# Storing two rows of the last tile in groups of partitions, so that one DMA engine takes half as many of them

## The chip, the cores and the metric

One core of a Trainium2 chip runs the whole kernel. The metric is the device time of one execution in microseconds (us); smaller is better. The kernel before took 3724.84 us (median of the fast runs). The profile counts 16 DMA engines for the core, whose packets move all the data between the chip's memory (HBM) and the core's own memory (SBUF): 1610.68 MB on the page of the kernel before.

## The reference

```python
# x, residual: (32, 2048, 2048) float32; gamma: (2048,), eps: a number
def reference(x, residual, gamma, eps):
    z = x + residual
    rms = np.sqrt(np.mean(z ** 2, axis=-1, keepdims=True) + eps)
    return (z / rms * gamma).astype(np.float32)
```

There are 65,536 rows of 8192 bytes. x and residual are read once and the result is written once: 1.61 GB.

## The kernel before

The rows are cut into tiles of 128 partitions times R = 7 rows (the first two tiles hold 3 and 5). SyncE's queue loads x and stores the results, ScalarE's queue loads the residual, VectorE adds and scales, ScalarE squares and sums. The last tile is done in four pieces of 2, 2, 2 and 1 rows, so that its stores can start early:

```python
    z = [sb(f"z{p}", [P, R, D]) for p in range(2)]
    tail = [(0, 2), (2, 4), (4, 6), (6, 7)]
    # ... (tiles, adds, squares, scaling)
    def sync_program(sp):
        # ... (loads and stores of all tiles but the stores of the last)
        for k, (a, b) in enumerate(tail):
            sp.wait_ge(tail_ev["done"], k + 1)
            sp.dma_start(
                out=rows(o_f, last)[:, a:b, :], in_=z[last % 2][:, a:b, :]
            ).then_inc(s_tail, U)
    # ...
    nc.gpsimd.wait_ge(ev["s_out"][(last - 1) % 2], ((last - 1) // 2 + 1) * U)
    nc.gpsimd.wait_ge(s_tail, U * len(tail))
    # ... (GpSimd clears the semaphores, and the program ends)
```

## Time and profile before

| | before |
|---|---|
| time, median | 3724.84 us |
| span of the profiled execution (which took 3725.53 us) | 3723.7 us |
| share of time in which the 16 DMA engines are busy | 100% |
| last 57344-byte packet of the second-last tile ends | 3705.04 us |
| last completion write of any engine | 3722.13 us |
| last of the 64 landings of the tail's stores | 3722.59 us |

The kernel is limited by the DMA engines from its first microseconds to about 3716 us. What can be gained at the end is the stretch in which engines fall idle one after another. The prediction below shows these lines of the profile and reads them. This is the view of all instructions that write the result tensor, from 3690 us on. After the name stand the count, the shortest, median and longest duration in ns, and the first and last start:

```profile
L269 SPq DMA_DIRECT2D out_dram<-z x4: 332/332/344, 3690.4 to 3708.8; - x4
```

### The profile page before, as it was taken

Reading aid. Unit: us, or ns where it says so; the run is one execution under the profiler, and the core shown is the slowest. Engines: PE = TensorE matmul, PEld = TensorE weight load, DVE = VectorE, ACT = ScalarE, POOL = GpSimd, SP = SyncE. Lnnn points to the kernel's source line nnn. Section 1 sums busy time; section 2 is a strip of 40 time slices with the busy share of each in tenths; the row PEclk is TensorE's granted clock in tenths of the full one; section 3 lists DMA queues with packets and bytes.
Section 4 is the critical chain, followed back from the end, with each engine's and each line's share of the span. In section 5 each row is a group of like instructions: output and inputs, shape, how many; then the busy total and the mean of one; then the engine's idle time right before and its main releaser. Section 6 shows DMA issues by size and latency. Waiting matters only on the chain.

```text
span 3723.7 us, 3798 instructions
## 1 busy us (share of the span) xinstructions
DVE 2302.6 (62%) x816; ACT 1072.4 (29%) x1176; POOL 0.2 (0%) x4
## 2 busy tenths in 40 slices
DVE  5666665566665566665566665566665566665566
ACT  2233322233322233322233322233322233322233
POOL 0000000000000000000000000000000000000000
DMA  9999999999999999999999999999999999999999
GB/s 421 431 434 435 434 434 435 434 435 435 434 434 434 434 434 434 434 434 433 434 434 434 434 434 434 434 434 434 434 434 434 434 434 434 434 434 434 434 432 398
DMA packets 32963, 1610.68 MB, mean 433 GB/s; under 512 B 3712, under 2 KB 3776, under 8 KB 3776
## 3 DMA queue, kind: packets, MB, share of 16 engines
q1 hardware_dynamic: 22592, 1082.17, 67.2%
q10 hardware_dynamic: 10368, 528.49, 32.8%
q14 instruction: 3, 0.02, 0.0%
HBM read 1073.77 MB, written 536.87 MB: 433 GB/s over the span
## 4 chain that ended last, share of the span: by engine, by line
DMA 67%; DVE 22%; issue 9%; ACT 2%; SPq 0%; DVEq 0%; ACTq 0%
DMA out_dram<-z 39%; DMA z<-in_x_dram 27%; DVE z L172 15%; DVE z L177 7%; ACT sq_junk L223 1%; ACT rms L231 0%; DVE rstd L197 0%; SPq L259 0%; DVEq L127 0%; DVE r_area L275 0%; ACTq L211 0%; ACTq L127 0%; SPq L141 0%; DVE tail_rstd L292 0%; SPq L162 0%
## 5 line engine op out<-in xcount | busy, mean ns | idle before, releaser
L172 DVE TENSOR_TENSOR z<-z,r_area 128x8192 f32<-128x8192 f32 (+2 forms) x150 | 1109.5, 7437 | 1252.5 <-DMA z<-in_x_dram 1252.5
L223 ACT ACTIVATE sq_junk<-z 128x2048 f32<-128x2048 f32 x512 | 963.4, 1882 | 2617.1 <-DVE z L172 2605.7
L177 DVE SCALAR_TENSOR_TENSOR z<-z,rstd,gamma_tile 128x2048 f32<-128x2048 f32 x505 | 1153.6, 2344 | 5.2
L197 DVE RECIPROCAL rstd<-rms 128x4 f32<-128x4 f32 (+2 forms) x146 | 25.3, 173 | 130.8 <-ACT rms L231 130.8
L223 ACT ACTIVATION_READ_ACCUMULATOR sq_junk<-z 128x1 f32 x512 | 95.5, 186 | 0.0
L231 ACT ACTIVATE rms<-ssq,eps_tile 128x4 f32<-128x4 f32 (+2 forms) x146 | 43.3, 297 | 13.4
L177 DVE SCALAR_TENSOR_TENSOR z<-z,tail_rstd,gamma_tile 128x2048 f32<-128x2048 f32 x7 | 16.2, 2345 | 0.1
L277 DVE LOAD_MASK_SELECT gamma_tile<-r_area x1 | 0.0, 14 | 16.1 <-DMA r_area<-in_gamma_dram 16.1
L277 DVE STREAM_SHUFFLE gamma_tile<-r_area 128x2048 f32<-128x2048 f32 x1 | 2.3, 2290 | 0.0
L275 DVE MEMSET r_area<- 128x2048 f32 x1 | 1.8, 1765 | 0.4 <-issue 0.4
L223 ACT ACT_TABLE_LOAD x1 | 1.3, 1283 | 0.9 <-SPq L77 0.9
L231 ACT ACT_TABLE_LOAD x1 | 1.3, 1283 | 0.1
L231 ACT ACTIVATE tail_rms<-tail_ssq,eps_tile 128x2 f32<-128x2 f32 (+1 forms) x4 | 1.2, 295 | 0.1
L274 DVE MEMSET eps_tile<- 128x1 f32 x1 | 0.1, 59 | 1.0 <-SPq L77 1.0
L292 DVE RECIPROCAL tail_rstd<-tail_rms 128x2 f32<-128x2 f32 (+1 forms) x4 | 0.6, 158 | 0.0
L349 POOL MEMSET const-bfloat16-1.0<- 128x1 bf16 x1 | 0.1, 101 | 0.0
L349 POOL MEMSET const-uint8-127<- 128x1 uint8 x1 | 0.1, 101 | 0.0
L349 POOL MEMSET const-float32-0.0<- 128x1 f32 x1 | 0.1, 98 | 0.2 <-issue 0.2
L349 POOL MEMSET const-float32-1.0<- 128x1 f32 x1 | 0.1, 98 | 0.0
## 6 DMA issues: line engine op xcount, KB each, us to landing
r_area<-in_residual_dram ACTq DMA_DIRECT2D x72, 7168.0 KB, 35.5
z<-in_x_dram SPq DMA_DIRECT2D x71, 7168.0 KB, 27.5
out_dram<-z SPq DMA_DIRECT2D x71, 7168.0 KB, 40.8
z<-in_x_dram SPq DMA_DIRECT2D x3, 2048.0 KB, 17.9
out_dram<-z SPq DMA_DIRECT2D x3, 2048.0 KB, 15.0
r_area<-in_residual_dram SPq DMA_DIRECT2D x1, 5120.0 KB, 25.0
z<-in_x_dram SPq DMA_DIRECT2D x1, 5120.0 KB, 36.7
out_dram<-z SPq DMA_DIRECT2D x1, 5120.0 KB, 26.5
```

The source lines that it names most:

```text
L172: return v.tensor_add(out=s, in0=s, in1=r_area[:, e + a : e + b, :])
L177: ins = v.scalar_tensor_tensor(out=s, in0=s, scalar=rs[:, c + g - a : c + g - a + 1], in1=gamma_tile[:, :], op0=mult, op1=mult,)
L197: v.reciprocal(out=rstd[p][h][:, :n], in_=rms[p][h][:, :n]).then_inc(dve, U)
L223: s.activation(out=sq_junk[:, :], in_=src[:, g, :], func=Act.Square, accum_out=sq[:, g - a : g - a + 1],)
L231: return s.activation(out=rm, in_=sq[:, : b - a], func=Act.Sqrt, bias=eps_tile[:, :], scale=inv_d)
L274: v.memset(eps_tile[:, :], float(eps))
L275: v.memset(stage, 0.0).then_inc(tail_ev["add"], 1)
L277: v.stream_shuffle(gamma_tile[:, :].rearrange("p (a b) -> p a b", a=16), stage, [0] * 32)
L292: v.reciprocal(out=tail_rstd[:, a:b], in_=tail_rms[:, a:b]).then_inc(dve, U)
L349: nc = _bacc.Bacc("TRN2", target_bir_lowering=False, num_devices=1)
```

## The change

One DMA engine ends some 3 us after all others (its last completion write is at 3722.13 us, that of any other at 3718.97 or before). The change takes work off it: rows 1 and 3 of the last tile are no longer stored over all 128 partitions. SyncE stores them for partitions 0 to 39 in ten small groups of 5, 4, 3 or 1 partitions, and GpSimd for 40 to 127 in two groups of 44. A small group runs on few engines: SyncE's load of k partitions has k landings, for k = 1 to 8. The trace doesn't number engines; number k - 1 in this document is the one that the load of k partitions adds. The sum is meant to give engine 4 eight rows less than it had. Two tiny loads on GpSimd's queue go ahead of its two stores.

```diff
+    tiny = sb("tiny", [8, 32])
+    soft = [sem(f"soft{k}") for k in range(4)]
 ...
-        for k, (a, b) in enumerate(tail):
+        for k, (a, b) in enumerate([(0, 1), (2, 3), (4, 6), (6, 7)]):
             sp.wait_ge(tail_ev["done"], k + 1)
-            sp.dma_start(
-                out=rows(o_f, last)[:, a:b, :], in_=z[last % 2][:, a:b, :]
-            ).then_inc(s_tail, U)
+            store_last(sp, slice(0, P), slice(a, b)).then_inc(s_tail, U)
+            if k == 1:
+                for q in low:
+                    store_last(sp, q, slice(1, 4, 2)).then_inc(s_tail, U)
+
+    low = [slice(k, k + 33, 8) for k in range(4)] + [slice(k, k + 25, 8) for k in range(4, 8)]
+    low += [slice(36, 39), slice(39, 40)]
+    high = [slice(k, P, 2) for k in (40, 41)]
+    n_tail = 4 + len(low)
+
+    def store_last(eng, q, r):
+        return eng.dma_start(out=rows(o_f, last)[q, r, :], in_=z[last % 2][q, r, :])
+
+    def pool_program(g):
+        def two_pairs(t, k):
+            return t[:5, 16 * k : 16 * k + 16].rearrange("p (a b) -> p a b", a=2)[:, :, :2]
+        for k in range(2):
+            g.dma_start(out=two_pairs(tiny, k), in_=two_pairs(x_f, k)).then_inc(soft[2 * k], U)
+            if k == 0:
+                g.wait_ge(tail_ev["done"], 2)
+            store_last(g, high[k], slice(1, 4, 2)).then_inc(soft[2 * k + 1], U)
+        for k in soft:
+            g.wait_ge(k, U)
+        g.dma_reset(range(soft[0].num, soft[-1].num + 1))
 ...
-    nc.gpsimd.wait_ge(s_tail, U * len(tail))
+    nc.gpsimd.wait_ge(s_tail, U * n_tail)
```

More of the change, by code (lines that the diff above doesn't have):

```diff
@@ L54 @@
     HI = LO + 2 * n_iter
-    assert n_iter >= 1
+    assert n_iter >= 1 and P == 128
     def rows(t, i):
@@ L326 @@
     scalar_program(nc.scalar)
+    pool_program(nc.gpsimd)
     nc.gpsimd.wait_ge(ev["s_out"][(last - 1) % 2], ((last - 1) // 2 + 1) * U)
-    nc.gpsimd.wait_ge(s_tail, U * len(tail))
+    nc.gpsimd.wait_ge(s_tail, U * n_tail)
     ids = [a.num for a in sems]
```

## The prediction

> **What bounds the kernel now.** I read the page first, then the busy time by stretches around the end, then the waits of SyncE's queue, then the single DMA packets and semaphore updates that the trace holds. The page's head, its DMA rows and its queues:
>
> ```profile
> span 3723.7 us, 3798 instructions
> DVE 2302.6 (62%) x816; ACT 1072.4 (29%) x1176; POOL 0.2 (0%) x4
> DMA  9999999999999999999999999999999999999999
> GB/s 421 431 434 435 434 434 435 434 435 435 434 434 434 434 434 434 434 434 433 434 434 434 434 434 434 434 434 434 434 434 434 434 434 434 434 434 434 434 432 398
> q1 hardware_dynamic: 22592, 1082.17, 67.2%
> q10 hardware_dynamic: 10368, 528.49, 32.8%
> ```
>
> No compute engine is near its limit, and the two queues together keep the 16 DMA engines 100.0% busy (67.2 + 32.8). The rate is flat at 434 GB/s and falls only in the last slice, to 398. So the kernel is a stream of 1610.68 MB, and all that a change of the last tile's stores can touch is that last slice. The view of the busy time in stretches opens it; its last two columns are the DMA share and GB/s:
>
> ```profile
> 3709.00:3714.00 5.00, 0.00 (x0) 0.00 (x0) 0.00 (x0) 1.00 0.98 419
> 3714.00:3716.00 2.00, 0.00 (x0) 0.00 (x0) 0.00 (x0) 1.00 0.98 418
> 3716.00:3717.00 1.00, 0.00 (x0) 0.00 (x0) 0.00 (x0) 1.00 0.82 344
> 3717.00:3718.00 1.00, 0.00 (x0) 0.00 (x0) 0.00 (x0) 1.00 0.37 156
> 3718.00:3719.00 1.00, 0.00 (x0) 0.00 (x0) 0.00 (x0) 1.00 0.18 74
> 3719.00:3720.00 1.00, 0.00 (x0) 0.00 (x0) 0.00 (x0) 1.00 0.08 33
> 3720.00:3722.00 2.00, 0.00 (x0) 0.00 (x0) 0.00 (x0) 1.00 0.06 25
> 3722.00:3724.00 2.00, 0.00 (x0) 0.00 (x0) 0.00 (x0) 1.00 0.00 0
> ```
>
> Compute has ended by 3709. Up to 3716 all 16 engines move data. By 3719 about three are left, and from 3720 to 3722 the share is 0.06, which is 1/16: **one engine works alone**. The semaphore updates of the last store say the same: eleven of its sixteen land from 3716.9 to 3717.9, four from 3718.8 to 3719.3, the last at 3722.59. The span ends 1.15 us after that. This engine is late all along, not only in the last store: its update trails the median by 2.2 us around 1600 us, by 4.3 us around 2820 us and by about 5 us in the tail, and its packets follow each other without a gap. It has its own queue of work and never starves, so its own sum of bytes sets the end.
>
> SyncE's queue in the last 224 us shows that issuing is not what the tail waits for; line 269 issues the four tail stores and waits for VectorE alone:
>
> ```profile
> SPq L162 <- DMA out_dram<-z: 42.8, 1, 42.8
> SPq L269 <- DVE z L177: 35.4, 4, 18.0
> ```
>
> The four issue at 3690.4, 3699.5, 3706.4 and 3708.8 and land a median 15.0 us later (1 MB: 13.8): data always lies queued ahead of them.
>
> [...]
>
> **The change part by part.** A unit is one row of one partition, 8192 bytes; such a packet takes 309 ns in the trace, and one of two rows 611 ns.
>
> *Removed.* The stores of rows 0-1 and 2-3 in packets of two rows: 8 + 8 packets for each engine, 16 x 0.611 = 9.78 us.
>
> *Added.* Rows 0 and 2 are stored over all 128 partitions: 8 + 8 units for each engine. Rows 1 and 3 were 16 units for each engine. [...]
>
> *Worth on each engine.* Engine 4: 24 x 0.309 = 7.42 us in place of 9.78, or **-2.36 us**. Engines 3 and 5-15: 32 x 0.309 = 9.89, +0.11 us, because the packets are smaller. Engine 2: +0.73; engines 0 and 1: 35 x 0.309 = 10.82, +1.04 us.
>
> *Where the end goes.* The last engine's final packet, the completion write, is at 3722.12. If it is engine 4 that is late, this becomes 3719.76. The four next-latest have theirs at 3718.45 to 3718.96; with engine 0 or 1 among them in the worst place, 3718.96 + 1.04 = 3720.0. So 3719.8 to 3720.0, middle 3719.9. From the completion write to the span's end it was 1.62 us, so the span becomes about 3721.5, and the measured time, 1.1 us longer than the span before (3724.84 against 3723.7), about **3722.6 us**: 2.2 us, 0.06%.
>
> *Issue cost.* SyncE issues ten more DMAs between the second and the third tail store. At 0.33 us (this line now) to 0.59 us (the gamma loads with 16 pieces) each that is 3.3 to 5.9 us, from 3699.8 to 3703.1-3705.7; the third store becomes due at 3706.4. Off the path. GpSimd issues two small loads (80 bytes of data each) and two stores. The first of each pair runs beside the main stream or just after 3699.4; the data isn't needed before the engines' backlog runs out, after 3709. Its reset and its waits come before the wait for the last store, which ends some 8 us later. Nothing on VectorE or ScalarE changes.
>
> **The rivals.**
> 1. *The late engine isn't number 4* (the trace doesn't number them). Then the late one gets +0.11 us (or up to +1.04 if it is 0 or 1), and the time is 3724.9 to 3725.9. For the change speaks that it is made for exactly this engine, and that the lateness is repeatable: the three times before lie within 0.15 us. I give this 0.12.
> 2. *GpSimd's path costs something new at the end*: [...] a GpSimd transfer split over engines in another way [...], or the reset outlasting the last store. Engines 5-15 have 1.7 to 2.8 us of room before 3719.8, GpSimd some 8 us. A small cost of 0.5 to 2 us is possible: 3723 to 3725. I give 0.2.
> 3. *SyncE's queue blocks.* Four x loads in a row at 3662.9 took 7.2 us to issue, one of them 4.6 us, while other transfers were queued. If the twelve stores block alike, the third store is issued late, at 3709 or 3710. Engines 5-15 still hold rows 1 and 3 from GpSimd then, so I expect it hidden; if not, 1 to 3 us are lost and the gain is gone. I give 0.1.
> 4. *More than the arithmetic:* no way past the four next-latest engines, so 3721.6 is about the floor.
>
> **Range and chances.** The arithmetic gives 3722.6. The rivals nearly all lie above it, so the range leans upward: 3721.6 to 3724.9. Two per cent would be 74 us; the whole last slice is 93 us and stays in place, so a change of over 2% either way would need a failure that nothing here points to: 0.005 each.
>
> **What would show it.** Right: the stretch with one engine alone (share 0.06) is gone or under 0.5 us, the share falls from 0.8 to 0.1 within about 3 us, a third DMA queue carries 88 partitions x 2 rows x 8192 B = 1.44 MB, SyncE's ten small issues end before VectorE has the third piece, and the span ends at 3721.3 to 3721.8. Wrong: one engine still works alone after 3720 with nothing shortened (it isn't number 4), or the share dips below 0.9 between 3700 and 3716 [...], or GpSimd's reset ends after the last landing. I would be wrong on the whole if using GpSimd's queue cost something at the start or the end of the program.

The forecast's sum came to 3722.6 us: the last completion write at 3719.76 (engine 4: 3722.12 - 2.36) to 3720.0 (another engine: 3718.96 + 1.04), middle 3719.9, then 1.62 to the span's end and 1.1 to the measured time. The estimate of the rows 0 to 3 on each engine: 35 on engines 0 and 1, 34 on 2, 32 on 3, 24 on 4 and 32 on each of the rest. The runs show this much of them: SyncE's loads of k = 1 to 8 partitions have k landings each (first probe run). The tail's semaphore has 115 updates in the changed kernel's trace: 64 of four whole stores and 51 of the ten small groups, which fits 4 x 5 + 4 x 4 + 3 + 2 = 41 landings and one update for each group that is none, as in the probes. The late engine's track has 24 packets of a row. And of GpSimd's 176 packets of 8192 bytes no more than 11 run at once, but for 0.16 us with 12. Which engines took GpSimd's packets isn't shown.

## The result, and the profile after

| | before | after |
|---|---|---|
| time, median of fast runs | 3724.84 us | 3727.40 us (3726.49 to 3728.49, 4 runs) |
| span of the profiled execution | 3723.7 us | 3725.2 us |
| last completion write of any engine | 3722.13 us | 3723.68 us |
| from the last landing to the span's end | 1.15 us | 1.17 us |

The changed kernel is 2.6 us slower, not 2.2 us faster. The ratio is 1.0007, with an interval of 0.999 to 1.0024, and the interval includes 1. That the changed kernel is slower at all rests on the ranges, which don't overlap here (before: 3724.69 to 3724.93) or in a later series. A ratio here is the mean time of one kernel's fast runs over that of the other's in the same rounds, so it is not quite the ratio of the medians. In that later series it took 3727.37 us (3726.47 to 3728.27) beside 3725.06 us (3724.89 to 3725.62).

The page of the changed kernel shows that GpSimd's queue (q0) did what it was given: 88 partitions x 2 rows x 8192 bytes are 1.44 MB. Its two stores and two tiny loads took 2.5 us of GpSimd in all:

```profile
span 3725.2 us, 3815 instructions
q0 software_dynamic: 352, 1.44, 0.1%
L286 POOL DMA_DIRECT2D out_dram<-z x2 | 1.3, 651 | 3697.1 <-DVE z L182 3697.1
L293 POOL DMA_DIRECT2D tiny<-in_x_dram x2 | 1.2, 624 | 1.1 <-PEq L392 1.1
```

The busy time by stretches of the changed kernel, with DMA share and GB/s in the last two columns, answers to the lines that the prediction shows of before:

```profile
3699.00:3706.00 7.00, 6.96 (x6) 2.30 (x3) 1.86 (x3) 1.00 0.95 382
3706.00:3709.00 3.00, 2.36 (x2) 0.00 (x0) 0.00 (x0) 1.00 0.95 336
3709.00:3714.00 5.00, 0.00 (x0) 0.00 (x0) 0.00 (x0) 1.00 0.52 179
3714.00:3716.00 2.00, 0.00 (x0) 0.00 (x0) 0.00 (x0) 1.00 0.99 389
3719.00:3720.00 1.00, 0.00 (x0) 0.00 (x0) 0.00 (x0) 1.00 0.92 385
3720.00:3722.00 2.00, 0.00 (x0) 0.00 (x0) 0.00 (x0) 1.00 0.51 213
3722.00:3724.00 2.00, 0.00 (x0) 0.00 (x0) 0.00 (x0) 1.00 0.07 29
```

The kernel before in one of these stretches, which the prediction doesn't show:

```profile
3706.00:3709.00 3.00, 2.77 (x3) 0.00 (x0) 0.00 (x0) 1.00 1.02 437
```

Two things are to be seen. First, there is a **hole** from 3709 to 3714: half of the engines have nothing to do. The view of the stores shows where it comes from:

```profile
L286 SPq DMA_DIRECT2D out_dram<-z x14: 332/783/2637, 3690.0 to 3712.8; - x14
```

An issue took 0.78 us in the median and up to 2.64 us, in place of 0.33. By the trace, the eleven stores from row 2 to the last small group took SyncE from 3699.05 to 3712.2 (the expectation of the third run below calls them twelve), and the store of rows 4 and 5, due when VectorE finished them at 3705.9, went out at 3712.24. The engines that don't serve the small groups ran dry before that: eleven of them start on rows 4 and 5 at 3713.3 and are done at 3720.8, some 3.5 us later than before.

Second, from 3706 to 3709 the engines are as busy as ever (0.95), but they move only 336 GB/s: 354 for a full share (336 / 0.95), where the kernel before moves 428 (437 / 1.02). **Busy engines are slower.** The single packets tell the same. Before, and at nearly all places, a packet of 8192 bytes takes 309 ns. In the changed kernel's tail, 75 of 640 such packets take over 320 ns, up to 1241 ns; the time over 309 ns adds up to 19.7 us over the engines. (An expectation below says 20.7; that sum comes out against 307.5 ns.)

The late engine can be followed through this, packet by packet. The trace doesn't number engines, but the late one's last 57344-byte packet is the last of all to end, and from there each next packet starts within 0.06 us of the end of the one before, with the sizes in the order of the issues (before: 24 packets of 16384 bytes, then 8 of 8192). For the changed kernel the track ends in the last completion write of all:

```
late engine, us        start    rows 0-3 done     rows 4-6   last write   run
before                3705.04    +9.77              +7.31     3722.12    17.08
changed               3704.66   +11.69 (8.59+3.10)  +7.32     3723.67    19.01
predicted, changed               +7.42 (4.95+2.47)  +7.31                14.72
```

In brackets stand rows 0 and 2 (16 packets) and the small groups (8 packets). It does carry 24 packets of a row, as predicted, but they took 11.7 us and not 7.4. Of the 4.3 us too many, 3.6 fell on rows 0 and 2, which are whole stores (8.59 in place of 4.95), and 0.6 on its own small groups (3.10 in place of 2.47). So what it lost, it lost mostly while its own stores were whole ones and other engines were storing groups. Rows 4 to 6, whole stores that it starts after the small groups, took what they took before.

### The profile page after: what moved, and what is told of

It is laid out like the page before. It is cut to its first block, busy times and chain, and to the rows that moved or that the text cites. A ratio compares the mean times of both kernels' runs of the same rounds, so it can differ in the third digit from the quotient of the medians.

```text
span 3725.2 us, 3815 instructions
## 1 busy us (share of the span) xinstructions
DVE 2302.6 (62%) x816; ACT 1072.4 (29%) x1176; POOL 2.7 (0%) x8
## 3 DMA queue, kind: packets, MB, share of 16 engines
q0 software_dynamic: 352, 1.44, 0.1%
## 4 chain that ended last, share of the span: by engine, by line
DMA 67%; DVE 22%; issue 9%; ACT 2%; SPq 0%; DVEq 0%; ACTq 0%
DMA out_dram<-z 39%; DMA z<-in_x_dram 27%; DVE z L177 15%; DVE z L182 7%; ACT sq_junk L228 1%; ACT rms L236 0%; DVE rstd L202 0%; SPq L264 0%; DVEq L132 0%; DVE r_area L303 0%; ACTq L216 0%; ACTq L132 0%; SPq L146 0%; DVE tail_rstd L320 0%; SPq L167 0%
```

## The experiments

The theories at the start were two. **Wrong engine:** the late engine is not number 4, so it got more rows and not fewer. **Blocked queue:** it is number 4 and was relieved, but SyncE's slow issue starved the rest. A third came out of the packets above, **choice of partitions:** which partitions the groups take decides how far packets are stretched. The expectations from the changed kernel's second timing on call it the shared-partition theory; that engines share partitions is an assumption in that name, for no trace here shows which partitions an engine reads.

### Which engine is late: probes behind the last store

```diff
+        for k in range(1, 17):    # behind the last store; sixteen tiles, sixteen semaphores
+            sp.dma_start(out=probes[k - 1][:, :], in_=x_f[:k, :17]).then_inc(s_probe[k - 1], U)
```

> The kernel before, and behind its last store SyncE issues sixteen small loads of k = 1 to 16 partitions (68 bytes each), each with its own semaphore and tile (probe_a is k = 1, probe_p is k = 16). If a load of k partitions runs on engines 0 to k-1 behind their queued stores, a load that includes the late engine lands only after about 3722.2 us, one without it within some 2 to 3 us of its issue or when the last of its other engines is done (by 3719.5). Wrong-engine theory: the first load that lands after 3722 is k = 1 or 2 (late engine 0 or 1; at most k = 4). Blocked-queue theory, which takes the late engine to be number 4: k = 1 to 4 land by 3719.5, and k = 5 is the first that lands after 3722. If none up to k = 15 lands late, it is engine 15. The span grows by 1 to 10 us for the probes; that means nothing.

Measured: the semaphore updates of the first eight probes in the trace (us). Each has one update more than the one before, and the new one is marked; the first update of each, 0.1 to 0.2 us after the end of the issue, is left out, for the load of k = 16 has none, so it is no landing.

```
k=1  *3716.26
k=2   3716.44 *3717.14
k=3   3716.62  3717.31 *3718.32
k=4   3716.80  3717.48  3718.45/3718.50 (one new)
k=5   3716.97  3717.65  3718.65  3718.70 *3722.19
k=6  *3716.72  3717.14  3717.82  3718.83  3718.86  3722.37
k=7  *3716.58 ...                                  3722.57
k=8  *3716.60 ...                                  3722.76
```

The first that lands late is k = 5 (3722.19 us, its other four landings by 3718.70), and each load has one landing more than the one before. By the numbering that this gives, the late engine is number 4, as the change has it, and the **wrong-engine theory is refuted**. The probes also show engines 2 and 3 behind the rest by 1 to 2 us, and 0 and 1 not.

> The changed kernel with the same sixteen probes behind its last store. The first probe that lands with the last engine (about 3723.7 to 3724) should be the same k as in the probe of the kernel before under both theories, if the late engine is a property of the core. Wrong-engine theory: k = 1 or 2, and it is the same engine that ended last in the profile of the changed kernel. Blocked-queue theory: k = 5.

The same probes in the changed kernel were less clear. The first updates of engines 0 to 4 came at about 3723.0, 3723.1, 3722.6, 3721.7 and 3723.5 us: number 4 is still the last, but 0 to 2 are within a microsecond of it, so "the first k that lands late" says little here. Before, engine 4 was over 3 us behind any other.

### The small groups issued last

```diff
-            if k == 1:
-                for q in low:
-                    store_last(sp, q, slice(1, 4, 2)).then_inc(s_tail, U)
+        for q in low:             # behind the store of row 6
+            store_last(sp, q, slice(1, 4, 2)).then_inc(s_tail, U)
```

> The changed kernel, but SyncE issues its ten small groups behind the last whole store, so their slow issue (13.2 us for the run of twelve stores in the changed kernel's profile) can't delay the stores of rows 4 to 6. Blocked-queue theory: the hole of 3709 to 3714 (DMA share 0.52) is filled, the eleven quick engines end near 3717 instead of 3720.8, and the time falls to 3722.6 to 3723.5. Wrong-engine theory: the hole is filled too and the quick engines end early, but the late engine still carries 19 rows in place of 16 and never ran dry, so the time stays within 1 us of the changed kernel's 3727.4 (3726.4 to 3728.4).

3726.56 us (3726.38 to 3726.75) beside 3725.01 us before. The hole is filled, yet the time is nearly that of the changed kernel. The number lies in the band that I had written for the wrong-engine theory, but that theory is out, so the hit is one by number alone. In this kernel the small groups end last: they are issued until 3720.96, and the last write, at 3723.36, comes behind packets of the last ones, of up to 979 ns.

```profile
3709.00:3714.00 5.00, 0.00 (x0) 0.00 (x0) 0.00 (x0) 1.00 1.00 390
3716.00:3717.00 1.00, 0.00 (x0) 0.00 (x0) 0.00 (x0) 1.00 0.87 303
3717.00:3718.00 1.00, 0.00 (x0) 0.00 (x0) 0.00 (x0) 1.00 0.41 131
3718.00:3719.00 1.00, 0.00 (x0) 0.00 (x0) 0.00 (x0) 1.00 0.51 164
```

From 3717 to 3719 GpSimd's data and the whole stores of the quick engines are done. What runs is mostly SyncE's small groups, and a full share of that would be only 320 GB/s (131 / 0.41, 164 / 0.51). So these groups seem to hold each other up without any help from GpSimd. The packets say more. Before SyncE issues its first small group, at 3708.44, 14 packets beside whole stores and GpSimd's groups already take over 320 ns, up to 756 ns, and nine of them are GpSimd's: its groups take part in the stretching too. And engine 4's rows 0 and 2, now without SyncE's groups beside them for most of the time, took 5.72 us in place of 8.59.

### Only whole stores, only smaller packets

```diff
-        for k, (a, b) in enumerate(tail):
+        for k, (a, b) in enumerate([(0, 1), (2, 3), (4, 6), (6, 7)]):
 ...                                # and behind (2, 3):
+                sp.dma_start(
+                    out=rows(o_f, last)[:, 1:4:2, :], in_=z[last % 2][:, 1:4:2, :]
+                ).then_inc(s_tail, U)
```

> The kernel before with rows 0, 2 and then 1 and 3 together as three whole stores of 128 partitions from SyncE, 16 rows on every engine, no GpSimd DMA and no small groups: only the packet size (8192 in place of 16384 bytes) and one more DMA. Both theories: +0.1 us (32 x 0.309 us in place of 16 x 0.611 us), 3724.8 to 3725.2. If it is over 1 us longer, the packet size or the order costs more than worked out, and both theories are incomplete.

3725.14 us (3724.84, 3725.06, 3725.23 and, in the profiled execution, 3727.68) beside 3725.01. This is in the expected band. None of its 640 packets of 8192 bytes took over 309 ns. In the profiled execution the late engine's tail began 2 us later than elsewhere, at 3707.19, before this engine moved anything of the new stores; from there it ran 17.12 us (before: 17.08). Packet size and one more store cost nothing that counts.

### The same sizes of SyncE's groups, other partitions

The next kernel keeps the sizes of SyncE's ten groups and picks other partitions for them. GpSimd's two stores change in size as well: they take 77 and 11 partitions in place of 44 and 44. I picked the partitions by an idea of which ones an engine serves in a whole store and what follows if engines share them. No run shows the theory, and its bands are named here where a result is held against them. The expectations call this kernel the own-partition version, after that idea; here it is the other-partition version.

```diff
-    low = [slice(k, k + 33, 8) for k in range(4)] + [slice(k, k + 25, 8) for k in range(4, 8)]
-    low += [slice(36, 39), slice(39, 40)]
-    high = [slice(k, P, 2) for k in (40, 41)]
+    low = [slice(k, k + 17, 4) for k in range(4)] + [slice(k, k + 13, 4) for k in range(32, 36)]
+    low += [slice(48, 51), slice(31, 32)]
+    high = [slice(51, 128), slice(20, 31)]
```

> The first probe says that the late engine is number 4, so the wrong-engine theory is out. The changed kernel's own packets show a new thing: from the stores of rows 1 and 3 on, packets of 8192 bytes took 400 to 1240 ns in place of 309 (20.7 us in sum over the engines), and whole stores alone show none. [...] Engine-sum theory of my prediction (only rows an engine count): 3722.3 to 3723.2. Theory of small groups or GpSimd costing by themselves: no change against the changed kernel, 3726.5 to 3728.5.

3724.11 us (3723.15 to 3724.97) beside 3724.82: 0.7 us less than before, with ranges that overlap (3724.47 to 3725.49), and 3.3 us under the changed kernel, which was timed in another call. It fell between the bands of the cut theory (3724.5 to 3725.6) and of my engine sum (3722.3 to 3723.2). Engine 4's run fell to 15.5 us, with rows 0 and 2 at 5.06 us (16 x 0.309 = 4.94) and the small groups at 3.06 (8 x 0.309 = 2.47). So engine 4 is relieved in this kernel, where the theory had expected no relief.

> The same, with the group of partitions 48 to 50 left out, so the result is wrong on purpose (six rows of the last tile are not stored). Engine 4's own work is unchanged; only engines 0 to 2, which do not end last, do 2 rows less each. [...]

The result is wrong; six rows are not stored. 3723.61 us (3723.06 to 3724.37): 0.5 us under the run with them, with overlapping ranges, so the times decide nothing. In the trace engine 4's small groups took 2.52 us in place of 3.06 and its run 14.90 us in place of 15.51, though its own work is the same. That is one execution each. It hints that a small group without engine 4 (k = 3 reached engines 0 to 2 in the first probe run) can still stretch engine 4's packets, and shows no more. Two bands: 3722.8 to 3724.2, and at least 0.8 us under the run with the six rows, for the theory; the same as that run within 0.4 us for all others. The theory wanted up to 1.8 us off engine 4; it was 0.6.

### Groups of 16 partitions, without GpSimd

```diff
-                sp.dma_start(out=rows(o_f, last)[:, 1:4:2, :], ...)       # of the whole-store run
+                for g in range(8):
+                    q = slice(g, P, 8)                    # or: slice(16 * g, 16 * g + 16)
+                    sp.dma_start(out=rows(o_f, last)[q, 1:4:2, :], in_=z[last % 2][q, 1:4:2, :])
```

> No GpSimd DMA and equal work: rows 0 and 2 as whole stores, rows 1 and 3 as eight SyncE groups of 16 partitions with step 8, [...] Small-group theory: eight more DMAs cost their issue only; the same as the run with blocks of 16, packets of 309 ns.

> The same as the step-8 run but for which partitions a group takes: eight groups of 16 neighbouring partitions. [...] Small-group theory: the same time as the step-8 run within 0.5 us and packets of 309 ns.

Step 8: 3730.24 us (3729.83 to 3730.64). Blocks of 16: 3729.59 us (3728.28 to 3732.92). Before: 3724.82. So rows 1 and 3 in eight groups of 16 partitions, meant as equal loads, without GpSimd and without relief for anyone, cost 5 us, where whole stores cost nothing. The small-group theory had packets of 309 ns. Summed over the engines, the time over 309 ns is 46 us with step 8 and 80 us with blocks, and the longest packet 1361 and 2378 ns, so it is refuted. Cut from the expectations are the bands of the theory named above, 3727 to 3730 for step 8 and 3730 to 3740 for blocks, the blocks later: both results lie just outside, and that order came in the packets and not in the times. From 3709 to 3714, in the step-8 run and then in the run with blocks:

```profile
3709.00:3714.00 5.00, 0.00 (x0) 0.00 (x0) 0.00 (x0) 1.00 0.79 202
```

```profile
3709.00:3714.00 5.00, 0.00 (x0) 0.00 (x0) 0.00 (x0) 1.00 0.89 167
```

A full share is worth 256 GB/s (202 / 0.79) with step 8 and 188 (167 / 0.89) with blocks, against 428 before. The blocks don't end later as well: engine 4 ran 22.3 us with step 8 and about 20.2 with blocks, where its track is less sure. A possible reason is that it comes to its groups late, when the others are mostly through theirs; no run tests this.

### All again on one chip, and the small groups from ScalarE

> The changed kernel again, beside the kernel before on the same chip as the next three, because it and the own-partition version were timed in different calls. Shared-partition theory (the choice of partitions stretches packets): again 1 to 3 us over the kernel before, 3726 to 3728.5. If it is chance of a call: within 0.5 us of the kernel before.

> The own-partition version again. Engine 4's packets in its first profile ran 15.5 us from the end of the big store to its last completion write (before: 17.1, changed: 19.0), so its own sum did fall; [...] Shared-partition theory in its weaker form: 3723 to 3725 again, 2 to 4 us under the changed kernel. If it is chance: like the changed kernel.

> The own-partition version a second time on this chip, one look with a profile only: does engine 4's run of 15.5 us repeat? If yes, 15.0 to 16.2 us from the end of the big store to its last completion write, and the third store is issued about 2.4 us after VectorE is done with its piece.

The third of these is, in spite of its label, the other-partition kernel a second time. Beside the kernel before at 3725.06 us (9 runs, 3724.89 to 3725.62), the changed kernel took 3727.37 us (3726.47 to 3728.27) and the other-partition version 3723.63 us (3722.99 to 3724.54; the extra look 3724.08). No ranges of the three kernels overlap. In the two other-partition runs the third store went out 2.3 and 2.6 us after VectorE was done with its piece, as expected. Engine 4 ran 19.7 us in the changed kernel and 15.4 and 15.3 us in the other. In the other-partition kernels the track could be confused with a neighbour's; the last write of any engine bounds its run by 15.5, 16.0 and 15.4 us.

```
late engine, us                start   rows 0 and 2   small groups   rows 4-6   run
changed, again                3704.39     8.30           4.08          7.31    19.69
other partitions              3704.35     5.06           3.06          7.39    15.51
other partitions, again       3705.16     5.07           2.96          7.36    15.39
other partitions, third look  3705.38     5.05           2.91          7.38    15.34
other partitions, 6 rows less 3704.41     5.06           2.52          7.32    14.90
```

The stretching isn't gone from this kernel. Over all engines its packets of 8192 bytes ran 9.7, 12.1 and 11.7 us over 309 ns in the three looks, beside 19.7 and 14.7 us in the two of the changed kernel; single ones took up to 2138 ns. What changed clearly is engine 4: 8.0 to 8.1 us for its 24 packets, beside 11.7 and 12.4.

The second run of the other-partition version ends like this. By the track engine 4 is done at 3720.56, and another engine writes last, at 3721.15:

```profile
3706.00:3709.00 3.00, 2.81 (x3) 0.00 (x0) 0.00 (x0) 1.00 1.00 393
3709.00:3714.00 5.00, 0.00 (x0) 0.00 (x0) 0.00 (x0) 1.00 0.80 283
3718.00:3719.00 1.00, 0.00 (x0) 0.00 (x0) 0.00 (x0) 1.00 0.98 410
3719.00:3720.00 1.00, 0.00 (x0) 0.00 (x0) 0.00 (x0) 1.00 0.35 148
3720.00:3722.00 2.00, 0.00 (x0) 0.00 (x0) 0.00 (x0) 1.00 0.07 29
```

There is still a hole (0.80) in it, since SyncE's issues still delay the third store. Does that cost time?

```diff
         for k, (a, b) in enumerate([(0, 1), (2, 3), (4, 6), (6, 7)]):      # SyncE
 ...
-            if k == 1:
-                for q in low:
-                    store_last(sp, q, slice(1, 4, 2)).then_inc(s_tail, U)
 ...
+        s.wait_ge(tail_ev["done"], 2)                                      # end of ScalarE's program
+        for q in low:
+            store_last(s, q, slice(1, 4, 2)).then_inc(s_tail, U)
```

> The own-partition version with the ten small groups issued by ScalarE, at the end of its program, in place of SyncE. Blocked-queue theory for what is left (the small groups held up SyncE's third store by 2.4 us and the quick engines ended at 3718.6 in place of 3717): the third store is issued as soon as VectorE is done, the quick engines end near 3717, and the time is 3722.3 to 3723.5. If SyncE's queue isn't what is left: the same as the own-partition version, 3723.2 to 3725.

3724.01 us (3723.37 to 3724.47): no better than with SyncE (3723.63), and out of the band of the blocked-queue theory. Yet what it was aimed at is gone: SyncE's three stores go out when VectorE is done with their pieces, and the share stays near 1 until 3716, with most of the quick engines done between 3716.2 and 3717.7.

```profile
3709.00:3714.00 5.00, 0.00 (x0) 0.00 (x0) 0.00 (x0) 1.00 0.94 379
```

```profile
3698.55 9.70 SPq L283 DMA_DIRECT2D out_dram<-z  x3
3702.86 12.31 ACTq L283 DMA_DIRECT2D out_dram<-z  x10
```

The last two are from the timeline (start and extent, both in us). ScalarE now needs 12.3 us for the ten small issues. The run doesn't test the hole alone: the small groups start some 3 us later than from SyncE (3702.86; 3699.88 in the second other-partition run), and the last four completion writes, up to 3720.10, are all of ScalarE's queue, so the small groups now end last.

That **starving the quick engines is real but did not set the end** of the changed kernel is read from its own two traces. The late engine had work without a gap over 0.06 us up to the last write of all. And in the second trace the third store was 4.5 us late in place of 6.3, and the share from 3709 to 3714 was 0.78 in place of 0.52, while the late engine's run was longer (19.7 us in place of 19.0).

## Why the prediction was wrong, point by point

- *What bounds the kernel, and that only the last slice counts:* right. But for one tiny load at the start, every kernel here differs from the one before only in the last 30 us.
- *The late engine is number 4* (rival 1 gave 0.12 to the contrary): right; the first probe run shows it (k = 5 lands at 3722.19 us, k = 1 to 4 by 3718.50).
- *Rows on each engine: 24 for engine 4:* right as counts. GpSimd's queue moved 1.44 MB, and the late engine's track has eight packets in four small groups.
- *"Engine 4: 24 x 0.309 = 7.42 us in place of 9.78, or -2.36 us":* **this is the step that failed.** The 24 packets took 11.69 us, so the gain of 2.36 became a loss of 1.92 (11.69 - 9.77), 4.3 us off. I took the duration of a packet where all 16 engines do whole stores and held it fixed while others store groups. Most of the loss, 3.6 us, came on rows 0 and 2, which stayed whole stores, and not on the small groups. With SyncE's groups on other partitions the same sum holds to 0.6 to 0.8 us (15.3 to 15.5 us of run against 14.72), and with 6 rows left out to 0.2. That the choice of partitions does it is shown by the other-partition version beside the changed kernel on one chip, 3723.63 against 3727.37 us (only GpSimd's split, 77 and 11 for 44 and 44, changed with it). Whole stores without one stretched packet, and groups of 16 that lose 5 us, fit it. How it does it is not shown: no trace has the partitions that an engine reads, and a partition's rows also have their own place in HBM, and no run moves one without the other.
- *"SyncE issues ten more DMAs ... 3.3 to 5.9 us ... Off the path":* wrong in size. The ten small stores took 12.8 us (3699.42 to 3712.19), and the third store was 6.3 us late. Rival 3, which had this, reckoned with "hidden, or 1 to 3 us lost". The hole came, but the late engine had work all along.
- *GpSimd's path costs little:* right for its issue and its reset, not for its data. The reset took 83 ns at 3713.9 us, ten microseconds before its last wait ended, and no more than eleven of its data packets run at once but for 0.16 us with twelve, which fits eleven engines for 44 partitions. Its data did take part in the stretching: 27 of the 75 stretched packets are its own, and with SyncE's groups behind the last store it stretched packets before any of them was issued.
- *From the last write to the span's end 1.62 us:* about right, 1.50. The 1.1 us that the prediction adds after it is the median less the span of an execution that was 0.7 us slower than the median; span and time of one execution are 1.8 us apart. For a difference of medians that cancels.
- *The range:* all the rivals that I sized kept packets at 309 ns, so none reached 3727.

Set together for the two profiled executions: the late engine's tail began 0.4 us earlier (3704.66 against 3705.04), ran 1.9 us longer (19.01 against 17.08) and was followed by 0.1 us less; the span grew by 1.4 us (3725.17 against 3723.74). The medians lie 2.6 us apart, because the profiled execution of before was 0.7 us slower than its median and the one of after 0.4 us faster.

The other-partition version lies under both, by 1.4 us under the kernel before (0.7 in the first) and 3.7 us under the changed one on the same chip. That is still 1.0 to 1.5 us above the predicted 3722.6. Its ratio to the kernel before is 0.9996 with an interval of 0.9982 to 1.0009.

## What to carry to other kernels

Before work is moved from one DMA engine to another, look at what the groups do to the stores that run beside them. As far as these runs go: time more than one choice of partitions for the same groups, for two choices lay 3.7 us apart here (3723.63 and 3727.37), and look at GB/s per share of busy time, for a share of 0.95 moved only 336 GB/s here. A late engine can be found with small probe loads of k = 1 to 16 partitions behind the last store, as k = 5 found it here at 3722.19 us. And many small DMAs in a row can hold up the queue that issues them: ten took 12.8 us here, where one whole store is issued in 0.33.
